# Rows of the split activations at one start modulo 256 bytes, in a hybrid decoder step on one core

## The chip, the cores and the metric

The kernel runs on one core of one Trainium2 chip. The metric is device time in microseconds (us), the median of several runs of one program. Engines are named as in the profile: PE is TensorE (matmuls), PEld its weight loads, DVE VectorE, ACT ScalarE, POOL GpSimd, SP SyncE, which here only issues DMAs.

## What is computed

The reference is one step of a decoder layer for 256 prompt tokens and 8 sample tokens (one new token of each of 8 requests), which share all weights. Everything is float32. Cut to its projections, it is:

```python
proj = rms_norm(x, g_mix) @ w_in                      # 2048 -> 6656: q, k, v, z, xBC, dt
attn = window_attention(q, k, v, sinks)               # window 128, 16 heads of 64, 4 kv heads
ssd  = rms_norm(scan(conv(xBC), dt) * silu(z), norm_g)
x = x + concat([attn, ssd]) @ w_out                   # 3072 -> 2048
x = x + cross_attention(x, memory) @ w_co             # 4 heads of 128 over 256 memory tokens
u = conv3(rms_norm(x, g_ffn) @ w_up)                  # 2048 -> 2 x 5632
x = x + (silu(gate(u)) * value(u)) @ w_down           # 5632 -> 2048
```

It also returns the new states and caches (keys, values, convolution rows, the scan's state).

## The kernel before, in words

**Layout.** Activations are kept transposed: 128 features in the partitions, and the T = 264 tokens (256 prompt, 8 sample) along the row. A block of 128 features is one row of 264 floats, 1,056 bytes. Eight such rows make a tile of 8 x 264 floats, 8,448 bytes, which `T3` allocates.

**Split operands.** A float32 product is computed as three matmuls of the type float32r. Each operand is split in a high half (a copy rounded to that type) and a low half (what is left). For weights this is done in `weights`: SP loads 1,024 columns of raw weights (`wraw`, 512 KB), ACT makes `whi` (L85), DVE makes `wlo` (L86). For activations `split` does it, with ACT and DVE (L93 without a gain, L94 and L95 with one). `mm3` issues the three matmuls: high weights with the high row (L100), high weights with the low row (L101), low weights with the high row (L102). The weights are the stationary operand, 128 columns, and the row of 264 tokens is the moving one.

**The loop.** `proj` takes weights of 8 feature blocks a unit, in two parts. Within a part it goes over the output blocks m (two, in some stages four), and for each over the rows k of the part, three matmuls each. With two output blocks a part has four rows: the order is rows 0 to 3 for m = 0, rows 0 to 3 for m = 1, then rows 4 to 7 for both.

**The stages**, in the order of PE's work: an opening written out by hand (L240), in which PE takes 4 output blocks at once, so that one row is the moving operand of 4 matmuls in a row, or of 8 with its low half; the input projections, with attention and scan between them; the output projection over the attention rows (`AT`) and the scan rows (`Y`); queries, memory keys and memory values; `w_co`; and the feed-forward stage, in which the up-projection (`up`, rows `X2`) runs one group of 8 blocks ahead of the down-projection (`down`, rows `H`). In the opening, rows 0 to 5 of a pass come one by one (four matmuls with the high half, four with the low half, both on high weights, then four with the high half on low weights), and later rows in pairs.

**Where the rows lie.** The split activations live in the pool `apool` under two tags of four buffers each, "A" and "B": xh, xl (input), yh, yl (scan output), ath, atl (attention output), x1h, x1l (for the queries), ohl (cross-attention output, high rows 0 to 3 and low rows 4 to 7 of one tile), x2h, x2l (up-projection), hh, hl (down-projection). In the built program all these buffers start at 192 modulo 256, because a buffer of 8,448 bytes is 33 x 256. A row is 4 x 256 + 32 bytes long, so the row k of a tile starts at 192 + 32k modulo 256. The buffers of `whi` and `wlo` start at 192 modulo 256 too, and a slice of 128 columns is 512 bytes.

The split memory rows (`mh`, `ml`, 256 tokens) are not under these tags: the first eight high rows are a T3 tile that starts at 192, with rows 1,056 bytes apart, and the other eight and all low rows are 1,024 bytes apart and start at 160 modulo 256.

**Software DMAs.** DMAs that POOL issues need a scratch in SBUF; the program reserves 16,384 bytes of each partition for it. POOL issues the loads of the samples' scan states (`h`, L868, three buffers) and of a broadcast (`cb`, L865) between 160 and 390 us, and the stores of new states (`hn`, L1333) in the feed-forward stage. All other DMAs are issued by SP.

**What sets the order.** A tile framework places the instructions on the engines by priorities, and the kernel pins some by `issue_after` and, in the opening, by hand.

Of the kernel before, what the change touches and what calls it, by code (L numbers as in the profile page):

```python
# [7 lines left out]
F32 = mybir.dt.float32  # L8
F32R = mybir.dt.float32r
# [6 lines left out]
KB = D // 128  # L16
TP, TS = 256, 8
T = TP + TS
EPS = 1e-6
DFF = 5632  # L20
FB = DFF // 128
# [26 lines left out]
def hybrid_decoder_step_kernel(ctx: ExitStack, tc: tile.TileContext, I, O):  # L48
    nc = tc.nc
# [4 lines left out]
    apool = ctx.enter_context(tc.tile_pool(name="apool", bufs=1))  # L54
# [7 lines left out]

    def T3(pool, n, dt=F32, tag=None, name=None, bufs=None):
        return pool.tile([128, n, T], dt, tag=tag, name=name or tag, bufs=bufs)


    NPART, WBUFS = 1024, 4
# [22 lines left out]
    def split(hi, lo, x, g=None):  # L90

        if g is None:
            return S.copy(out=hi, in_=x), V.tensor_tensor(out=lo, in0=x, in1=hi.bitcast(F32), op=ALU.subtract)  # L93
        return (S.activation(out=hi, in_=x, func=AF.Copy, scale=g),  # L94
                V.scalar_tensor_tensor(out=lo, in0=x, scalar=g, in1=hi.bitcast(F32), op0=ALU.mult, op1=ALU.subtract))  # L95
# [7 lines left out]

    def proj(units, acts, evac, n=T, nb=2, tag="mm"):

# [25 lines left out]
    par = cpool.tile([128, NPC], F32, name="par")  # L131
    cst = cpool.tile([128, NCST], F32, name="cst")
    hcol = cpool.tile([32, 2], F32, name="hcol")
    wdt = T3(apool, 8, F32, "C", "wdt").rearrange("p a t -> p (a t)")[:, 0:512].rearrange("p (k c) -> p k c", c=32)
    w_in = I["w_in"]
    small = ctx.enter_context(tc.tile_pool(name="small", bufs=2))
    A = []
    for h in range(2):
        A.append((T3(apool, 8, F32R, "A", f"xh{h}", 4), T3(apool, 8, F32R, "A", f"xl{h}", 4)))

# [1 line left out]
    op = oc.enter_context(tc.tile_pool(name="op", bufs=1))  # L144
    BLK = T + 512
    quarter = [op.tile([128, (KB if q == 0 else 0) + 4 * BLK], F32, name=f"open{q}") for q in range(4)]
# [9 lines left out]
    def x_of(k):  # L156
        return blocks[k // 4][:, k % 4, 0:T], gmix[:, k:k + 1]

# [12 lines left out]
    def w_piece(k, n):  # L171
        if k % 2 == 0:
            pre[k // 2] = [wpool.tile([128, NPART], F32R, tag=t, name=t, bufs=WBUFS).rearrange("p (k c) -> p k c", c=512)
                           for t in ("whi", "wlo")]
        return blocks[k // 4][:, k % 4:k % 4 + n, T:], *(w[:, k % 2:k % 2 + n, :] for w in pre[k // 2])

# [9 lines left out]

    acc0 = small.tile([128, T], F32, tag="acc", bufs=1, name="acc0")
    table = small.tile([128, 1], F32, tag="r", bufs=2, name="table")
# [74 lines left out]
    def pc(name, i=0, n=1):  # L263
        o = _PC[name][0]
        return par[:, o + i:o + i + n]
# [7 lines left out]
    eps = cpool.tile([128, 1], F32, name="eps")  # L273
    V.memset(eps, EPS)

# [9 lines left out]
    def sumsq(acc, x, first, w=T, on=P):  # L285
        if first:
            S.activation(out=acc, in_=x, func=AF.Square)
        else:
            sq = small.tile([128, T], F32, tag="sq", name="sq")
            S.activation(out=sq[:, :w], in_=x, func=AF.Square)  # L290
            on.tensor_tensor(out=acc, in0=acc, in1=sq[:, :w], op=ALU.add)
# [587 lines left out]
        V.tensor_tensor(out=x, in0=x, in1=pc("d_skip", 4 * g, 4).unsqueeze(2).broadcast_to([128, 4, 8]), op=ALU.mult)  # L879


    Y = [(T3(apool, 8, F32R, "B", f"yh{h}", 4), T3(apool, 8, F32R, "B", f"yl{h}", 4)) for h in range(2)]
    accy = small.tile([128, T], F32, tag="acc", bufs=1, name="accy")

    def z_pair(i):
# [9 lines left out]
        for m in range(2):  # L895
# [7 lines left out]
            sumsq(accy[:, :TP], y, k == 0, TP, V)  # L903
            split(Y[k // 8][0][:, k % 8, :TP], Y[k // 8][1][:, k % 8, :TP], y, gssd[:, k:k + 1])

    def gate_sample():
# [13 lines left out]
        for h in range(2):  # L920
            split(Y[h][0][:, :, TP:T], Y[h][1][:, :, TP:T], ysam[:, 8 * h:8 * h + 8, :])

# [26 lines left out]


    res_load()
    AT = (T3(apool, 8, F32R, "A", "ath", 4), T3(apool, 8, F32R, "A", "atl", 4))
    with tc.high_priority():
        for j in (0, 4):
            split(AT[0][:, j:j + 4, :], AT[1][:, j:j + 4, :], attn[:, j:j + 4, :])
    w_out = I["w_out"]

    for i in range(8):
        def ev(m, pm, i=i):
            k = 2 * i + m  # L960
            x = res[k // 4][:, k % 4, :]
            V.tensor_tensor(out=x, in0=pm, in1=x, op=ALU.add)
        proj([w_out[i]], [AT], ev, tag="t" if i % 2 else "mm")
        if i == 0:
# [51 lines left out]
    def mem_hl(k):  # L1016
        return mh[k // 8][:, k % 8, :TP], ml[k // 4][:, k % 4, :]

    X1 = [(T3(apool, 8, F32R, "A", f"x1h{h}", 4), T3(apool, 8, F32R, "A", f"x1l{h}", 4)) for h in range(2)]
    accx = small.tile([128, T], F32, tag="acc", bufs=1, name="accx")  # L1020
    for i in range(8):
        def ev(m, pm, i=i):
# [4 lines left out]
            V.tensor_tensor(out=x, in0=t, in1=x, op=ALU.add)  # L1027
            marks["x1"] = split(X1[k // 8][0][:, k % 8, :], X1[k // 8][1][:, k % 8, :], x, pc("g_cross", k))
        proj([w_out[8 + 2 * i], w_out[9 + 2 * i]], Y, ev, tag="t" if i % 2 else "mm")

# [44 lines left out]
    def q_pair(i):  # L1075
# [4 lines left out]

        proj([I["w_cq"][2 * i], I["w_cq"][2 * i + 1]], X1, ev)
        ms = slice(2 * i, 2 * i + 2)
# [162 lines left out]
    for b in range(6):  # L1245
        nc.sync.dma_start(out=va[b // 2][:, b % 2], in_=I["mv"][b])
        vts.append(va[b // 2][:, b % 2])
    OHL = T3(apool, 8, F32R, "A", "ohl", 4)
    OH, OL = OHL[:, 0:4, :], OHL[:, 4:8, :]
    sample_probs()  # L1250
    for b in range(6, 8):
# [13 lines left out]
            heads = out_head(2 * i + m)  # L1265
    nc.sync.dma_start(out=O["mem_v"], in_=vx)

    X2 = [(T3(apool, 8, F32R, "B", f"x2h{h}", 4), T3(apool, 8, F32R, "B", f"x2l{h}", 4)) for h in range(2)]
    accx2 = small.tile([128, T], F32, tag="acc", bufs=1, name="accx2")

    def x2_ev(k, pm):
        x = res[k // 4][:, k % 4, :]
        V.tensor_tensor(out=x, in0=pm, in1=x, op=ALU.add)
        split(X2[k // 8][0][:, k % 8, :], X2[k // 8][1][:, k % 8, :], x, pc("g_ffn", k))


    outs = [psum(t) for t in ("mm", "mm", "t", "t")]
    for pi, (wh, wl) in enumerate(weights(I["w_co"][0])):
        wh, wl = (w.rearrange("p (k c) -> p k c", c=512) for w in (wh, wl))
        for k in range(2):  # L1280
            h = 2 * pi + k
# [7 lines left out]
    for u in range(1, 4):  # L1289
        with tc.issue_after(heads[0].ins), tc.issue_after(heads[1].ins):  # L1290
            proj([I["w_co"][u]], [(OH, OL)], lambda m, pm, u=u: x2_ev(4 * u + m, pm), nb=4,
                 tag=[cyc[(4 * (u - 1) + m) % 5] for m in range(4)])
# [54 lines left out]
    w_up, w_dn = I["w_up"], I["w_dn"]  # L1347

    def up(g):
        H = (T3(apool, 8, F32R, "A", f"hh{g}", 4), T3(apool, 8, F32R, "A", f"hl{g}", 4))  # L1350
        n = len(groups[g])
        for ii, i in enumerate(groups[g]):
            us = []

            def ev(m, pm, i=i):
                bi = i + FB * m
                u = fp.tile([128, 2 + T], F32, tag="u", name="u", bufs=4)
                P.memset(u[:, 0:2], 0.0)
                ffn["ev"] = V.tensor_tensor(out=u[:, 2:], in0=pm, in1=r2, op=ALU.mult)
                us.append(u)  # L1360

            proj([w_up[2 * i], w_up[2 * i + 1]], X2, ev, tag="t" if i % 2 else "mm")
            cs = []
            for m in range(2):
                bi = i + FB * m
                u = us[m]
                ffn["new"] = P.tensor_copy(out=fnew[:, bi, :], in_=u[:, TP:])
                c = fp.tile([128, TP], F32, tag="c", name="c", bufs=4)
                w = [pc("fw", t * 88 + bi) for t in range(3)]
                ffn["c"] = S.activation(out=c, in_=u[:, 0:TP], func=AF.Identity, scale=w[0], bias=pc("fb", bi))  # L1370
                for t in (1, 2):
                    V.scalar_tensor_tensor(out=c, in0=u[:, t:t + TP], scalar=w[t], in1=c, op0=ALU.mult, op1=ALU.add)
                cs.append(c)
            if i < 4:
                past(i)
            if 4 <= i < 36:
                with tc.issue_after(ffn["ev"].ins), tc.issue_after(ffn["c"].ins):
                    new_state(i // 2 - 2, i % 2)
            S.activation(out=cs[0], in_=cs[0], func=AF.Silu)
            V.tensor_tensor(out=cs[1], in0=cs[0], in1=cs[1], op=ALU.mult)  # L1380
            split(H[0][:, ii, :TP], H[1][:, ii, :TP], cs[1])
        b0 = groups[g][0]
        sc = []
        for m in range(2):
            bi = b0 + FB * m
            t = fp.tile([128, 8, 8], F32, tag="sc", name="sc", bufs=4)[:, 0:n, :]
            P.tensor_tensor(out=t, in0=fnew[:, bi:bi + n, 2:10], in1=pc("fw", 2 * 88 + bi, n).unsqueeze(2).broadcast_to([128, n, 8]), op=ALU.mult)
            P.tensor_tensor(out=t, in0=t, in1=fpc[:, bi:bi + n, :], op=ALU.add)
            sc.append(t)
        S.activation(out=sc[0], in_=sc[0], func=AF.Silu)  # L1390
        V.tensor_tensor(out=sc[1], in0=sc[0], in1=sc[1], op=ALU.mult)
        split(H[0][:, 0:n, TP:T], H[1][:, 0:n, TP:T], sc[1])
        return H

    def down(g, H, last):
        if len(groups[g]) == 8:
# [3 lines left out]
        for src, nb, b0 in plan:  # L1400
            def ev(m, pm, b0=b0):
# [3 lines left out]
                if last:  # L1405
                    nc.sync.dma_start(out=O["y"][:, k, :], in_=x)
            proj([src], [H], ev, nb=nb)

# [148 lines left out]
def build(shapes):  # L1557

    import concourse.bacc as bacc

    nc = bacc.Bacc("TRN2", target_bir_lowering=False, num_devices=1)
    ins = {n: nc.dram_tensor(f"in_{n}_dram", s, dt, kind="ExternalInput").ap() for n, (s, dt) in shapes.items()}
    outs = {n: nc.dram_tensor(f"out_{n}_dram", s, F32, kind="ExternalOutput").ap() for n, s in _OUTS}
    with tile.TileContext(nc, schedule_with_timeline_sim=True) as tc:
        hybrid_decoder_step_kernel(tc, ins, outs)
    return nc
# [10 lines left out]
```

## Time and profile before

| | us |
|---|---|
| runs: median of 3 (lowest to highest) | 1399.39 (1399.31 to 1399.88) |
| profiled execution: span from the first to the last instruction | 1397.1 |
| PE busy (matmuls, 11,535) | 1392.5 |
| DVE busy | 1052.1 |
| ACT busy | 769.3 |
| POOL busy | 95.4 |

The profiled execution is an execution of its own; its span leaves out what lies before the first and after the last instruction, and the median of the runs is 2.3 us above it.

How to read the rows: a window's row has its bounds in us, its length, the engine's busy time with the number of instructions, the granted share of PE's clock, the mean busy share of the DMA engines, and GB/s. A row in order of time has the start in us, how long it took, engine, line, operation, output and inputs, the shape, and how many equal instructions it merges. A group's row has busy us and mean ns of one, then the idle time ahead of it and what ended that.

Successive matmuls overlap: one is marked as lasting some 284 ns, but the next starts some 121 ns after it did. What counts for time is the step from start to start, which is time divided by the number of starts.

### The profile page before, as it was taken

Reading aid. Unit: us, or ns where it says so; the run is one execution under the profiler, and the core shown is the slowest. Engines: PE = TensorE matmul, PEld = TensorE weight load, DVE = VectorE, ACT = ScalarE, POOL = GpSimd, SP = SyncE. Lnnn points to the kernel's source line nnn. Section 1 sums busy time; section 2 is a strip of 40 time slices with the busy share of each in tenths; the row PEclk is TensorE's granted clock in tenths of the full one; section 3 lists DMA queues with packets and bytes.
Section 4 is the critical chain, followed back from the end, with each engine's and each line's share of the span. In section 5 each row is a group of like instructions: output and inputs, shape, how many; then the busy total and the mean of one; then the engine's idle time right before and its main releaser. Section 6 shows DMA issues by size and latency. Waiting matters only on the chain.

```text
span 1397.1 us, 29012 instructions
## 1 busy us (share of the span) xinstructions
PE 1392.5 (100%) x11535; PEld 1367.8 (98%) x11535; DVE 1052.1 (75%) x1874; ACT 769.3 (55%) x1255; POOL 95.4 (7%) x286
## 2 busy tenths in 40 slices
PE   9999999999999999999999999999999999999999
PEld 9999999999999999899999999999999999999998
DVE  7879799999987774578777775777577757765654
ACT  7667756556545554566565544554455445543532
POOL 0000011121000000002010000000000000000000
PEclk9999999999999999999999999999999999999999
DMA  7954467777777567565576765676567656655664
GB/s 299 323 162 135 139 217 245 233 239 253 235 221 240 182 237 263 209 251 191 186 255 213 255 208 187 211 254 211 185 211 239 197 184 197 196 180 183 191 185 138
DMA packets 89479, 298.33 MB, mean 214 GB/s; under 512 B 12032, under 2 KB 17152, under 8 KB 88832
## 3 DMA queue, kind: packets, MB, share of 16 engines
q1 hardware_dynamic: 83840, 277.61, 60.5%
q0 software_dynamic: 5504, 18.88, 4.1%
q8 instruction: 90, 1.47, 0.4%
q14 instruction: 45, 0.37, 0.1%
HBM read 280.77 MB, written 16.23 MB: 213 GB/s over the span
## 4 chain that ended last, share of the span: by engine, by line
PE 100%; DVE 0%; issue 0%
PE mm L100 21%; PE mm L101 21%; PE mm L102 21%; PE t L100 10%; PE t L102 10%; PE t L101 10%; PE t L240 1%; PE y L825 1%; PE t L278 1%; PE y L841 0%; PE s L240 0%; PE mm L240 0%; PE x L278 0%; PE t L559 0%; PE x L1137 0%; PE s L1184 0%
## 5 line engine op out<-in xcount | busy, mean ns | idle before, releaser
L85 ACT CAST whi<-wraw 128x1024 fp32r<-128x1024 f32 x440 | 459.9, 1048 | 530.6 <-PE mm L101 278.3
L86 DVE TENSOR_TENSOR wlo<-wraw,whi 128x1024 fp32r<-128x1024 f32 x440 | 541.8, 1233 | 221.1 <-ACT whi L85 217.3
L100 PE MATMUL mm<-x2h,whi 128*128 128x264 f32 x704 | 199.8, 284 | 0.0
L100 PE MATMUL t<-x2h,whi 128*128 128x264 f32 x704 | 199.8, 284 | 0.0
L102 PE MATMUL t<-x2h,wlo 128*128 128x264 f32 x704 | 199.7, 284 | 0.0
L101 PE MATMUL mm<-x2l,whi 128*128 128x264 f32 x704 | 199.6, 284 | 0.0
L101 PE MATMUL t<-x2l,whi 128*128 128x264 f32 x704 | 199.5, 283 | 0.0
L102 PE MATMUL mm<-x2h,wlo 128*128 128x264 f32 x704 | 199.3, 283 | 0.0
L101 PE MATMUL mm<-hl,whi 128*128 128x264 f32 x704 | 198.7, 283 | 0.0
L102 PE MATMUL mm<-hh,wlo 128*128 128x264 f32 x704 | 198.2, 283 | 0.0
L100 PE MATMUL mm<-hh,whi 128*128 128x264 f32 x704 | 197.2, 284 | 0.0
L100 PE MATMUL mm<-xh,whi 128*128 128x264 f32 x576 | 164.7, 287 | 0.0
L101 PE MATMUL mm<-xl,whi 128*128 128x264 f32 x576 | 164.5, 287 | 0.0
L102 PE MATMUL mm<-xh,wlo 128*128 128x264 f32 x576 | 162.8, 287 | 0.0
L101 PEld LDWEIGHTS mm<-x2l,whi 128*128 128x128 f32 x704 | 132.6, 188 | 0.0
L100 PEld LDWEIGHTS t<-x2h,whi 128*128 128x128 f32 x704 | 132.5, 188 | 0.0
L101 PEld LDWEIGHTS t<-x2l,whi 128*128 128x128 f32 x704 | 132.5, 188 | 0.0
L101 PEld LDWEIGHTS mm<-hl,whi 128*128 128x128 f32 x704 | 132.4, 188 | 0.0
L100 PEld LDWEIGHTS mm<-x2h,whi 128*128 128x128 f32 x704 | 132.4, 188 | 0.0
L102 PEld LDWEIGHTS t<-x2h,wlo 128*128 128x128 f32 x704 | 132.2, 188 | 0.0
L102 PEld LDWEIGHTS mm<-x2h,wlo 128*128 128x128 f32 x704 | 132.1, 188 | 0.0
L102 PEld LDWEIGHTS mm<-hh,wlo 128*128 128x128 f32 x704 | 132.0, 188 | 0.0
(506 smaller groups left out, 2950.7 us busy)
## 6 DMA issues: line engine op xcount, KB each, us to landing
wraw<-in_w_up_dram SPq DMA_DIRECT2D x176, 512.0 KB, 4.4
wraw<-in_w_in_dram SPq DMA_DIRECT2D x96, 512.0 KB, 4.7
wraw<-in_w_dn_dram SPq DMA_DIRECT2D x88, 512.0 KB, 4.3
wraw<-in_w_out_dram SPq DMA_DIRECT2D x48, 512.0 KB, 4.4
h<-in_h_dram POOLq DMA_DIRECT2D x32, 256.0 KB, 4.6
hn<-in_h_dram SPq DMA_DIRECT2D x16, 512.0 KB, 4.8
out_state_s_dram<-hn POOLq DMA_DIRECT2D x16, 512.0 KB, 3.5
e<-dram_la SPq DMA_DIRECT2D x16, 256.0 KB, 5.5
```

Source lines behind the costliest of these rows:

```text
L85: S.copy(out=hi, in_=x)
L86: V.tensor_tensor(out=lo, in0=x, in1=hi.bitcast(F32), op=ALU.subtract)
L100: PE.matmul(out, wh, xh, start=start, stop=False)
L101: PE.matmul(out, wh, xl, start=False, stop=False)
L102: return PE.matmul(out, wl, xh, start=False, stop=stop)
L240: PE.matmul(first[c][:, :T], pre[k // 2][i][:, k % 2, c * 128:(c + 1) * 128], A[k // 8][x][:, k % 8, :], start=k + i + x == 0, stop=k == K ...
L278: return PE.transpose(out, in_, cst[0:k, C_ID:C_ID + k])
L825: PE.matmul(y[o:o + 64, (h // 2) * 128:(h // 2) * 128 + 128], xdt[:, h, :], es[h // 4][:, h % 4, :], start=True, stop=True)
```

## The change

Three edits:

- A helper `rows` takes the place of `T3` for all split activations under the tags "A" and "B". It allocates 8 rows of 320 floats, 1,280 bytes or 5 x 256, and hands out the first 264 of each. All rows of a tile now start at the same place modulo 256. A buffer grows from 8,448 to 10,240 bytes, eight buffers by 14,336 together. Other tiles under these tags (caches, flat scratch) keep their size and lie at the front of a buffer.
- An unused tile of 56 floats (224 bytes) is allocated first in `apool`, so that the buffers behind it, tag "C" among them, start at 160 modulo 256 in place of 192.
- The scratch of the software DMAs shrinks from 16,384 to 2,048 bytes a partition: 14,336 bytes, 56 x 256. The weight buffers therefore stay at 192 modulo 256.

In the built program every row of xh, xl, yh, yl, ath, atl, x1h, x1l, ohl, x2h, x2l, hh and hl starts at 160 modulo 256. Tiles that lie behind these buffers move down by 32 modulo 256 (the memory rows from 160 to 128). The instructions of every engine stand in the same order as before. Only four have another shape: the two splits of the attention rows write 4 rows of 264 on ACT and DVE where they wrote one run of 1,056.

```diff
+PITCH = 320
...
+    def rows(tag, name):
+        return apool.tile([128, 8, PITCH], F32R, tag=tag, name=name, bufs=4)[:, :, :T]
...
     hcol = cpool.tile([32, 2], F32, name="hcol")
+    apool.tile([128, 56], F32, tag="gap", name="gap")
     wdt = T3(apool, 8, F32, "C", "wdt").rearrange("p a t -> p (a t)")[:, 0:512].rearrange("p (k c) -> p k c", c=32)
...
-        A.append((T3(apool, 8, F32R, "A", f"xh{h}", 4), T3(apool, 8, F32R, "A", f"xl{h}", 4)))
+        A.append((rows("A", f"xh{h}"), rows("A", f"xl{h}")))
...
-    Y = [(T3(apool, 8, F32R, "B", f"yh{h}", 4), T3(apool, 8, F32R, "B", f"yl{h}", 4)) for h in range(2)]
+    Y = [(rows("B", f"yh{h}"), rows("B", f"yl{h}")) for h in range(2)]
...
-    AT = (T3(apool, 8, F32R, "A", "ath", 4), T3(apool, 8, F32R, "A", "atl", 4))
+    AT = (rows("A", "ath"), rows("A", "atl"))
...
-    nc = bacc.Bacc("TRN2", target_bir_lowering=False, num_devices=1)
+    nc = bacc.Bacc("TRN2", target_bir_lowering=False, num_devices=1, dynamic_dma_scratch_size=2048)
```

The same replacement is made for x1h and x1l, ohl, x2h and x2l, and hh and hl.

More of the change, by code (lines that the diff above doesn't have):

```diff
@@ L1017, in mem_hl @@
         return mh[k // 8][:, k % 8, :TP], ml[k // 4][:, k % 4, :]
-    X1 = [(T3(apool, 8, F32R, "A", f"x1h{h}", 4), T3(apool, 8, F32R, "A", f"x1l{h}", 4)) for h in range(2)]
+    X1 = [(rows("A", f"x1h{h}"), rows("A", f"x1l{h}")) for h in range(2)]
     accx = small.tile([128, T], F32, tag="acc", bufs=1, name="accx")
@@ L1247, in hybrid_decoder_step_kernel @@
         vts.append(va[b // 2][:, b % 2])
-    OHL = T3(apool, 8, F32R, "A", "ohl", 4)
+    OHL = rows("A", "ohl")
     OH, OL = OHL[:, 0:4, :], OHL[:, 4:8, :]
@@ L1266, in hybrid_decoder_step_kernel @@
     nc.sync.dma_start(out=O["mem_v"], in_=vx)
-    X2 = [(T3(apool, 8, F32R, "B", f"x2h{h}", 4), T3(apool, 8, F32R, "B", f"x2l{h}", 4)) for h in range(2)]
+    X2 = [(rows("B", f"x2h{h}"), rows("B", f"x2l{h}")) for h in range(2)]
     accx2 = small.tile([128, T], F32, tag="acc", bufs=1, name="accx2")
@@ L1349, in up @@
     def up(g):
-        H = (T3(apool, 8, F32R, "A", f"hh{g}", 4), T3(apool, 8, F32R, "A", f"hl{g}", 4))
+        H = (rows("A", f"hh{g}"), rows("A", f"hl{g}"))
         n = len(groups[g])
```

## The prediction

> **What bounds the kernel now.** I read the page first, then PE's waits, then the windows of the feed-forward stage, and last the single instructions in order of time.
>
> ```profile
> span 1397.1 us, 29012 instructions
> PE 1392.5 (100%) x11535; PEld 1367.8 (98%) x11535; DVE 1052.1 (75%) x1874; ACT 769.3 (55%) x1255; POOL 95.4 (7%) x286
> PEclk9999999999999999999999999999999999999999
> PE 100%; DVE 0%; issue 0%
> ```
>
> PE is busy for all of the span, the chain that ended last is PE alone, and the granted clock is in its top tenth in every slice. PE's waits are one row:
>
> ```profile
> PE x L201 <- DVE eps L274: 1.2, 1, 1.2
> ```
>
> So no transfer and no other engine holds PE back; only the pace at which matmul follows matmul counts. A row of the page does not give that pace, because matmuls overlap:
>
> ```profile
> L100 PE MATMUL mm<-x2h,whi 128*128 128x264 f32 x704 | 199.8, 284 | 0.0
> ```
>
> One takes 284 ns, but its successor starts long before it ends. The pace is time by count, over a window of the feed-forward stage in which PE runs nothing but matmuls of 264 columns (first row PE, second DVE, third DVE in the input projections):
>
> ```profile
> 650.00:1390.00 740.00, 740.00 (x6113) 1.00 0.63 204
> 650.00:1390.00 740.00, 512.01 (x833) 1.00 0.63 204
> 30.00:360.00 330.00, 300.92 (x638) 1.00 0.66 216
> ```
>
> 740.00 us over 6,111 starts (of the 6,113, two were already running at the window's edge) is 121.1 ns a matmul, at clock 1.00. DVE is busy for 69% of the first window, but for 91% of the second.
>
> **What each part costs.** Before, row k of an activation tile starts at 192 + 32k modulo 256, so rows 0 to 7 start at 192, 224, 0, 32, 64, 96, 128, 160, and every pass over a tile goes through all eight. After, every row starts at 160. The slices of the weights start at 192 modulo 256 in both kernels. The term that decides is therefore the pace of a stream whose rows all start at 160. The trace holds a small piece of it: in the opening (L240) row 7 is the moving operand of eight matmuls in a row, four of xh and four of xl, on four slices of weights. Two such pieces, the two halves of the opening:
>
> ```profile
> 15.41 0.41 PE L240 MATMUL t<-xh,whi 128*128 128x264 f32 x2
> 15.66 0.28 PE L240 MATMUL mm<-xh,whi 128*128 128x264 f32 x1
> 15.78 0.28 PE L240 MATMUL s<-xh,whi 128*128 128x264 f32 x1
> 15.90 0.40 PE L240 MATMUL t<-xl,whi 128*128 128x264 f32 x2
> 16.14 0.28 PE L240 MATMUL mm<-xl,whi 128*128 128x264 f32 x1
> 16.26 0.28 PE L240 MATMUL s<-xl,whi 128*128 128x264 f32 x1
> ...
> 27.08 0.41 PE L240 MATMUL t<-xh,whi 128*128 128x264 f32 x2
> 27.33 0.28 PE L240 MATMUL mm<-xh,whi 128*128 128x264 f32 x1
> 27.45 0.28 PE L240 MATMUL s<-xh,whi 128*128 128x264 f32 x1
> 27.57 0.40 PE L240 MATMUL t<-xl,whi 128*128 128x264 f32 x2
> 27.81 0.28 PE L240 MATMUL mm<-xl,whi 128*128 128x264 f32 x1
> 27.93 0.28 PE L240 MATMUL s<-xl,whi 128*128 128x264 f32 x1
> ```
>
> The first two steps after row 6 take 0.25 us together in both pieces (15.41 to 15.66, 27.08 to 27.33): an entry. The five steps behind it take 0.60 us in both, 120.0 ns each, unbroken by the change from xh to xl in their middle. Another start in the same opening gives another pace; row 4, which starts at 64, has eleven steps from its first to its twelfth matmul:
>
> ```profile
> 11.50 0.42 PE L240 MATMUL t<-xh,whi 128*128 128x264 f32 x2
> ...
> 12.86 0.29 PE L240 MATMUL s<-xh,wlo 128*128 128x264 f32 x1
> ```
>
> 1.36 us over 11 is 123.6 ns. I take it from these rows that the start does matter, that a stream which stays at 160 settles at 120.0 ns, and that the entry is paid only where the start changes. After the change it no longer changes.
>
> **The pace rule of the Trainium skill.** Its page "TensorE: Matmul & The Clock Gate", section "Back-to-back issue gap", puts matmuls in a stream N / 2.4 + 2.5 ns apart when warm, with no term for where a row starts. For 264 columns that is 112.5 ns by estimate; this trace has 121.1, so the measurement decides on the size. By that formula the pace term would be zero.
>
> *The sum.* Matmuls of 264 columns outside the opening: up-projection 88 blocks x 16 rows x 3 = 4,224, down-projection 44 x 16 x 3 = 2,112, input projections 48 x 16 x 3 = 2,304, output projection 16 x 24 x 3 = 1,152, query projection 4 x 16 x 3 = 192, w_co 16 x 4 x 3 = 192: 10,176. Each gains 121.1 - 120.0 = 1.1 ns, in all 11.2 us. The opening's own 192 I leave out; its first matmuls keep the pace of the loads. The sum is made on the profiled execution: 1397.1 - 11.2 = 1385.9 us of span. The median of the runs, 1399.39, lies 2.3 us above that span, and I carry this over: 1388.2 us.
>
> *Its bounds.* A start is printed to 0.01 us, so ten steps in 1.20 us are 118.6 to 121.4 ns, a gain of 25 us at one end and a loss of 3 at the other. I take the middle, because two pieces 12 us apart agree. The 2,304 matmuls of the input projections are the least sure, since DVE is already busy 91% of that stretch: if DVE became late there, their 2.5 us would be lost. In the feed-forward stage DVE's cover is 31% and PE gains 1%, so it stays hidden; DMA is busy for 0.63 there.
>
> *The splits of the attention rows (L955, recorded as L93).* Two ACT and two DVE instructions now write four rows of 264 with gaps, where each wrote 1,056 in one run.
>
> ```profile
> L93 ACT CAST ath<-attn x2: 1072/1072/1072, 358.4 to 359.4; 128x1056 fp32r<-128x1056 f32 x2
> L93 ACT CAST hh<-c 128x256 fp32r<-128x256 f32 x44 | 17.7, 402 | 1.3 <-DVE c L1380 1.3
> ```
>
> As four separate copies of nearly a row they would take 4 x 402 = 1,608 ns, so the break between rows costs from nothing to 0.5 us each, on engines that PE does not wait for. I take nothing, with 2 us if all four were exposed. All other writers already write one row, or the eight sample columns of each.
>
> *The scratch.* It shrinks from 16,384 to 2,048 bytes a partition. The software queue carries what POOL issues and nothing else: 32 loads and 8 of 256 KB and 16 stores of 512 KB make its 18.9 MB.
>
> ```profile
> q0 software_dynamic: 5504, 18.88, 4.1%
> L868 POOL DMA_DIRECT2D h<-in_h_dram x32 | 17.4, 543 | 141.1 <-DVE ych L870 100.6 <-PE mm L102 20.4 <-DVE cnew L741 18.6
> DMA to landing us min/median/max: 3.6/4.6/7.0
> DVE h L869: 0.6, 1
> ```
>
> POOL already stands still for 141.1 us until a tile h is free, and three such tiles exist, so at most three of these loads are open at a time, next to one of cb. If each of the 32 also had to wait for its forerunner to land, that would be 32 x 4.6 = 147 us, nearly all of it inside the 141.1 that POOL waits anyway; up to 6 us could reach DVE, which takes h, with the low halves of the weights queued behind it. DVE waited 0.6 us for h in all. I take nothing and keep 6 us for the range. No gain comes from here.
>
> **The rivals.**
>
> *A, the forecast:* the stream settles at 120.0 ns; 1388.2 us; chance 0.62. By the parts above its own range is 1380 to 1396.
>
> *B, the start is not the cause.* The steps would differ by their order in the pass, and their mean would be kept. The memory-key projection speaks for this. It streams 256 columns; its first 48 matmuls take their high halves from rows at eight different starts, the next 48 have every operand's rows at 160. Its first matmul, the first on the second tile, and the first of the next stage:
>
> ```profile
> 510.01 0.28 PE L100 MATMUL mm<-mh,whi 128*128 128x256 f32 x1
> ...
> 515.69 0.28 PE L100 MATMUL mm<-mh,whi 128*128 128x256 f32 x1
> ...
> 521.37 0.29 PE L100 MATMUL mm<-x1h,whi 128*128 128x264 f32 x1
> ```
>
> 5.68 us over 48 is 118.3 ns, 5.68 over 48 the same. Against it: those rows are shorter and end elsewhere, and a third of the first 48, the low halves, start at 160 too. It gives 1399.4; chance 0.19. The Trainium skill's page "SBUF — State Buffer", section "Specifications (TRN2)", says that memory lines have 16 bytes and that two hits a line keep full bandwidth. By that rule all starts here, multiples of 32 bytes, would be alike, and the time B's; the two paces of the opening, 120.0 and 123.6, do not fit it.
>
> *C, 160 is a bad start inside a projection.* In the feed-forward stage row 7's three matmuls are high, low, high, on changing weights, and one visit is slow:
>
> ```profile
> 705.81 0.29 PE L100 MATMUL mm<-x2h,whi 128*128 128x264 f32 x1
> 705.94 0.28 PE L101 MATMUL mm<-x2l,whi 128*128 128x264 f32 x1
> 706.06 0.28 PE L102 MATMUL mm<-x2h,wlo 128*128 128x264 f32 x1
> 706.18 0.28 PE L100 MATMUL mm<-x2h,whi 128*128 128x264 f32 x1
> ```
>
> 0.37 us over three is 123.3 ns. If that were the pace of every row, not the price of coming from row 6, the loss would be 2.2 x 10,176 = 22 us, 1421.8. With half of the visits at the mean it is 11 us, 1410.6, which I give for C. It decides where the settled pace at 160 lies above 121.1. Against it stand the five even steps of 120.0; chance 0.19. A scratch that makes POOL late would add its 6 us here.
>
> **How the numbers follow.** The likeliest case gives 1388.2. The range takes A from 1380 (a pace of 119.2) and B whole, and reaches 1406, the near part of C; most of C and a tail of A are left out, near 2 in 10. A measurement of this kernel can tell about 0.2%, 2.8 us, from no change: A is faster, B the same, C slower, which gives 0.62, 0.19 and 0.19.
>
> **What would show it.** Right: the window 650 to 1390 counts about 6,167 matmuls (740 / 0.120), all steps alike in runs, and the gain grows evenly along PE's stream, 7 us of it in the feed-forward stage. B: still 6,113. C: fewer, about 6,060. DVE waiting for h, or PE waiting for low halves of weights between 160 and 400 us, would show the scratch. It is wrong if the pace moves in the up-projection alone, since all stages share the starts.

## The result, and the profile after

| | before | after |
|---|---|---|
| runs, median of 5, us (lowest to highest) | 1399.48 (1399.31 to 1399.88) | 1388.36 (1387.37 to 1388.79) |
| profiled execution, span, us | 1397.1 | 1386.1 |

The ratio is 0.992, 95% interval 0.9908 to 0.9932: 11.1 us less, where 11.2 were forecast. The page of the changed kernel:

```profile
span 1386.1 us, 29012 instructions
PE 1381.1 (100%) x11535; PEld 1355.9 (98%) x11535; DVE 1050.2 (76%) x1874; ACT 768.4 (55%) x1255; POOL 96.7 (7%) x286
PEclk9999999999999999999999999999999999999999
PE 97%; DVE 1%; DMA 1%; ACT 1%; issue 0%; SPq 0%; ACTq 0%; DVEq 0%
```

The same instructions ran at the same clock, and the other engines were busy as long as before, to within 2 us; PE's busy time fell by 11.4 us. The chain that ended last is no longer PE alone: 3% of it now goes over DVE, DMA and ACT.

The windows, PE first and DVE second, of the feed-forward stage and of the stretch with the input projections (the feed-forward window ends at 1380, since this kernel's last matmul starts at 1382.45):

```profile
650.00:1380.00 730.00, 730.00 (x6086) 1.00 0.63 206
650.00:1380.00 730.00, 508.16 (x827) 1.00 0.63 206
30.00:360.00 330.00, 301.24 (x640) 1.00 0.67 218
```

730 us over 6,084 starts (two were already running at the edge) is 119.99 ns a step; the kernel before has 6,031 in the same window, 121.1 ns:

```profile
650.00:1380.00 730.00, 730.00 (x6031) 1.00 0.64 205
```
The steps themselves, in order of time in the up-projection:

```profile
700.02 0.28 PE L104 MATMUL mm<-x2h,whi 128*128 128x264 f32 x1
700.13 0.28 PE L105 MATMUL mm<-x2l,whi 128*128 128x264 f32 x1
700.25 0.28 PE L106 MATMUL mm<-x2h,wlo 128*128 128x264 f32 x1
700.38 0.28 PE L104 MATMUL mm<-x2h,whi 128*128 128x264 f32 x1
...
701.10 0.28 PE L104 MATMUL mm<-x2h,whi 128*128 128x264 f32 x1
```

They repeat every three matmuls, 0.36 us, whichever row, weights or output block it is: nine steps in 1.08 us. Before, the step depended on the place in the pass, as in the 0.37 us that the prediction shows for row 7's three.

Where the gain lies is read from the same landmark in both traces. The rows are the chain's first group behind the opening, the first matmul of the output projection, the first of the feed-forward stage, and the last matmul. Of the kernel before:

```profile
29.19 1.93 PE x L247 x32
362.95 0.41 PE L100 MATMUL mm<-ath,whi 128*128 128x264 f32 x2
625.82 0.29 PE L100 MATMUL mm<-x2h,whi 128*128 128x264 f32 x1
1393.43 0.28 PE L102 MATMUL mm<-hh,wlo 128*128 128x264 f32 x1
```

and of the changed one:

```profile
28.91 1.92 PE x L252 x32
360.72 0.40 PE L104 MATMUL mm<-ath,whi 128*128 128x264 f32 x2
621.71 0.36 PE L104 MATMUL mm<-x2h,whi 128*128 128x264 f32 x1
1382.45 0.28 PE L106 MATMUL mm<-hh,wlo 128*128 128x264 f32 x1
```

0.3 us were gained in the opening, 3.8 from there to the feed-forward stage (2.0 of them in the input projections), and 6.9 in it. The 0.3 in the opening are not shown to be the rows' doing, since run 1 below, whose rows lie as before, has them too:

```profile
28.91 1.93 PE x L247 x32
```

### The profile page after: what moved, and what is told of

Read it like the earlier page. It is cut to its first block, busy times and chain, and to the rows that moved or that the text cites. A ratio compares the mean times of both kernels' runs of the same rounds, so it can differ in the third digit from the quotient of the medians.

```text
span 1386.1 us, 29012 instructions
## 1 busy us (share of the span) xinstructions
PE 1381.1 (100%) x11535; PEld 1355.9 (98%) x11535; DVE 1050.2 (76%) x1874; ACT 768.4 (55%) x1255; POOL 96.7 (7%) x286
## 4 chain that ended last, share of the span: by engine, by line
PE 97%; DVE 1%; DMA 1%; ACT 1%; issue 0%; SPq 0%; ACTq 0%; DVEq 0%
PE mm L105 21%; PE mm L106 21%; PE mm L104 21%; PE t L105 10%; PE t L106 9%; PE t L104 9%; PE t L245 1%; PE t L283 1%; PE y L830 1%; PE y L846 0%; DMA e<-dram_la 0%; DMA open<-in_open_dram 0%; PE mm L245 0%; PE s L245 0%; PE t L564 0%; PE x L1142 0%
## 5 line engine op out<-in xcount | busy, mean ns | idle before, releaser
L104 PE MATMUL mm<-x2h,whi 128*128 128x264 f32 x704 | 196.5, 279 | 0.0
L104 PE MATMUL t<-x2h,whi 128*128 128x264 f32 x704 | 196.4, 279 | 0.0
L104 PE MATMUL mm<-hh,whi 128*128 128x264 f32 x704 | 194.1, 280 | 0.0
```

Of the source, the lines that this page charges most:

```text
L104: PE.matmul(out, wh, xh, start=start, stop=False)
```

## The experiments

The prediction left open what in the starts matters. The theories tested:

- **S**: each start has a settled pace of its own, which can be read from a few matmuls in the opening. This is the step on which the forecast rests.
- **O**: one start for all rows is what counts, whichever it is.
- **R** against **A2**: what counts is the row's start relative to that of the weights, or the row's own.
- **L**, formed after the first four runs: a stream with one start locks into a repeating cycle of steps; several cycles exist, 120.0 ns is the fastest, and a slower one can hold until PE pauses.

All paces below are from the window 650 to 1380 (two instructions less than its count), where PE runs nothing but matmuls of 264 columns.

**1. The scratch alone.**

```diff
-    nc = bacc.Bacc("TRN2", target_bir_lowering=False, num_devices=1)
+    nc = bacc.Bacc("TRN2", target_bir_lowering=False, num_devices=1, dynamic_dma_scratch_size=2048)
```

> The kernel before, with the smaller scratch alone; every row starts where it did modulo 256. If the gain is the pace of the matmuls, nothing moves: 1399.5 us, 121.1 ns a step in the feed-forward stage. If the scratch has any part in the time, by POOL's loads or by where tiles lie in memory, the time leaves 1399.5 by more than 1 us; the full gain would be 1388.4.

```profile
650.00:1380.00 730.00, 730.00 (x6030) 1.00 0.64 205
```

1399.34 us, ratio 1.0 (0.9991 to 1.0009), 121.1 ns. The scratch has no part in the time that shows, to 0.1%.

**2. The gap alone.** The scratch is small (run 1's edit), the gap is there, rows stay 1,056 bytes apart.

```diff
+    apool.tile([128, 56], F32, tag="gap", name="gap")
```

> The kernel before with the gap and the smaller scratch, rows still 1,056 bytes apart: a tile goes through the same eight starts, rotated by one (160, 192, 224, 0 and then 32 to 128). Both theories of the pace (each start has its own; or only the change from start to start costs) expect the mean over all eight to stay: 121.1 ns, 1399.5 us, at most 3 us from it, since the rows that follow each other at the ends of a part are others. If the gap as such is the gain, 1388.

```profile
650.00:1380.00 730.00, 730.00 (x6040) 1.00 0.64 206
```

1397.8 us, ratio 0.999 (0.9981 to 1.0), 120.9 ns. Rotating the eight starts moves the mean by 0.2 ns. The gap alone is not the gain.

**3. Rows at 192: the change without its gap.**

```diff
-    apool.tile([128, 56], F32, tag="gap", name="gap")
```

> The change without its gap: rows 1,280 bytes apart, all at 192 modulo 256. Theory S (each start has a settled pace of its own): in the opening of the kernel before, row 0 of the second half took 0.60 us over the five steps from 17.61 to 18.21, 120.0 ns, so 1388, within 6 us for the rounding of the rows. Theory O (one start for all is what counts, whichever): 1388.4, the time of the changed kernel. This run alone does not part them; it tells whether 160 is needed.

The ten executions fall into two groups: five from 1389.96 to 1391.16 and five from 1398.63 to 1400.05 (the profiled one, at 1400.05). Median 1394.9, ratio 0.9965 (0.9944 to 0.9985), which describes neither group.

```profile
650.00:1380.00 730.00, 730.00 (x6019) 1.00 0.64 205
```

In the profiled execution, of the slower group, the pace is 121.3 ns. No trace of the other group was kept; that its pace is lower is read from its time alone. One program then has two paces, so one start does not have one settled pace: S and O both miss. The gap is needed if every execution is to have the gain. L was formed on this and the next run.

**4. Rows at 64.**

```diff
-    apool.tile([128, 56], F32, tag="gap", name="gap")
+    apool.tile([128, 32], F32, tag="gap", name="gap")
```

> The changed kernel with a gap of 128 bytes in place of 224: all rows at 64 modulo 256. Theory S: row 4 in the opening of the kernel before, which starts there, had 123.6 ns a step over eleven steps, so 2.5 ns over the mean of 121.1, times 10,176 is 25 us more than before: 1425 us, slower than before. Theory O: 1388.4, like 160. Theory B of the prediction (starts do not matter) has fallen with the result, unless it was the distance and not the start.

1393.16 us, ratio 0.9957 (0.9942 to 0.9972): 32 us less than S had forecast, 5 more than O. The stage changes its pace within itself. It begins at 73 starts in 9 us, 123.3 ns, close to the 123.6 of row 4 in the opening. At 641.40 two matmuls with other operands (L300, a sum for the norm) stand in the stream; the next two rows begin 0.25 and 0.56 us behind that, and a few matmuls later the stream runs at 120.0:

```profile
630.00:639.00 9.00, 9.00 (x75) 1.00 0.70 226
650.00:1380.00 730.00, 730.00 (x6086) 1.00 0.64 206
```

The timeline at the change of pace, in which the second row is the break:

```profile
641.27 0.29 PE L105 MATMUL t<-x2l,whi 128*128 128x264 f32 x1
641.40 0.61 PE L300 MATMUL y<-accx,cst 128*128 128x264 f32 x2
641.65 0.48 PE L106 MATMUL t<-x2h,wlo 128*128 128x264 f32 x1
641.96 0.28 PE L104 MATMUL t<-x2h,whi 128*128 128x264 f32 x1
```

**5. Rows at 192 and weights at 224.** A tile of 32 bytes ahead of the weights moves them by 32; the gap of 224 behind them brings the rows back to 192.

```diff
+    cpool.tile([128, 8], F32, name="wgap")
     apool.tile([128, 56], F32, tag="gap", name="gap")
```

> Rows at 192 as in the run without the gap (which fell into two groups, five executions near 1390 and five near 1399), but the weights moved from 192 to 224 modulo 256, so that rows and weights stand to each other as in the changed kernel (rows 32 bytes behind). Theory R (what counts is the start of the moving row relative to the weights that load beside it): the changed kernel's time in every execution, 1388.4, 120.0 ns a step. Theory A2 (what counts is the row's own start): again two groups, 1390 and 1399.

```profile
650.00:1380.00 730.00, 730.00 (x6086) 1.00 0.64 206
```

1387.18 us in the median of executions from 1386.92 to 1388.29, ratio 0.9914 (0.9899 to 0.9929), 120.0 ns. The rows start where run 3 had them; of the operands of the projections, only the weights moved, by 32 bytes. Four executions could miss a slower group (1 chance in 16 at run 3's shares), but all four also lie below run 3's faster group, which begins at 1389.96. R fits this, A2 does not. It is the only place where one relative start was tried at two absolute ones.

**6. Two starts in turn: rows 1,152 bytes apart, at 160 and 32.**

```diff
-PITCH = 320
+PITCH = 288
```

> Rows 1,152 bytes apart (4.5 x 256), so that they start at 160 and at 32 in turn. If a change of start costs an entry at each row (the prediction's reading): at least the mean of the kernel before, 121.1 ns and 1399.5 us, since the start changes as often as there and 12.5 ns of entry over six steps would make it 122. If any short repeating pattern of starts locks into a cycle at the floor of 120.0: 1388.4.

```profile
650.00:1380.00 730.00, 730.00 (x6028) 1.00 0.64 205
```

1399.85 us, ratio 1.0005 (0.9995 to 1.0014), 121.1 ns, the time of the kernel before. Half of the rows at 160 bring nothing, with the other half at the start that run 12 shows to be the slowest. With run 12 (all rows at 32, 126.7 ns), the mean of the two single paces would be 123.3; the pair takes 121.1, so paces of starts do not add up.

**7. Rows at 128.** The gap has 48 floats.

> Gap of 192 bytes, all rows at 128. Theory S (settled pace read in the opening of the kernel before, here 14.69 to 15.29, 0.60 us over five steps): 120.0 ns, 1388. Theory L (one start for all locks the stream into some cycle; 120.0 is the fastest, slower ones exist and hold until PE pauses): 1388 to 1393, by stage 120.0 or a steady slower value such as the 121.3 and 123.3 that rows at 192 and 64 showed; never a changing mean like 121.1 of eight starts.

```profile
650.00:1380.00 730.00, 730.00 (x6085) 1.00 0.64 206
```

1390.65 us, ratio 0.9938 (0.9923 to 0.9952), 120.0 ns here. The 2.3 us over the changed kernel lie ahead of this window: the profiled execution begins its feed-forward stage at 624.79, the changed kernel's at 621.71. L's range holds it, S's point lies 2.7 us below.

**8. Rows at 96.** The gap has 40 floats.

> Gap of 160 bytes, all rows at 96. The opening of the kernel before had 122.7 ns a step there (12.98 to 14.33, eleven steps). Theory S: 1.6 ns x 10,176 = 16 us over before, 1416. Theory L: stages at 120.0 and stages at a steady slower value near 122, so between 1388 and 1409; in the feed-forward stage 120.0 once PE has paused.

```profile
650.00:1380.00 730.00, 730.00 (x6002) 1.00 0.64 205
```

1404.97 us, ratio 1.0039 (1.0024 to 1.0054): one start for all rows, and slower than eight. The pace is 121.7 ns; the same two matmuls of L300 stand in this stream (at 643.07) and did nothing to it: 74 starts in the 9 us from 630 are 121.6 ns. That goes against L's guess of 120.0 behind them.

**9. Rows at 224.** The gap has 8 floats.

> Gap of 32 bytes, all rows at 224, 32 bytes ahead of the weights modulo 256. Theory S: in the opening of the kernel before row 1, which starts there, took 1.10 us over the nine steps from 7.24 to 8.34, 122.2 ns: 1.1 x 10,176 = 11 us over before, 1411. Theory L (a cycle is steady, which one depends on start and on how the stream began): each stage at 120.0 or at one steady slower value, so 1388 to 1411, and the feed-forward stage at one value from its first pause on.

```profile
650.00:1380.00 730.00, 730.00 (x5975) 1.00 0.63 204
```

1409.51 us, ratio 1.0071 (1.0058 to 1.0085), 122.2 ns, as S read it in the opening.

**10. Rows at 0.** The gap has 16 floats.

> Gap of 64 bytes, all rows at 0, 64 bytes ahead of the weights. Theory S: row 2 in the opening of the kernel before, 8.84 to 9.92, 1.08 us over nine steps, 120.0 ns with an error of 1 ns: 1388, within 11. Theory L: each stage at 120.0 or at one steady slower value; 1388 to 1400.

```profile
650.00:1380.00 730.00, 730.00 (x6037) 1.00 0.64 206
```

Two groups again, four executions from 1390.17 to 1391.16 and six from 1395.71 to 1397.79; median 1396.01, ratio 0.9963 (0.9949 to 0.9976). The profiled one, of the second group, has 121.0 ns.

**11. The memory rows at one start.** In the changed kernel, with the first eight high rows of the memory 1,024 bytes apart and at 128, like its other memory rows.

```diff
-    mh = [T3(apool, 8, F32R, "C", "mh0"), xp.tile([128, 8, TP], F32R, name="mh1")]
+    mh = [T3(apool, 8, F32R, "C", "mh0").rearrange("p a t -> p (a t)")[:, 56:2104].rearrange("p (k t) -> p k t", t=TP), xp.tile([128, 8, TP], F32R, name="mh1")]
```

> The changed kernel with the first eight high rows of the memory 1,024 bytes apart and at 128, like the other memory rows there (64 bytes behind the weights). In the changed kernel the second 48 matmuls of the memory keys, whose rows all start at 128, step at 113 to 114 ns, the first 48, whose high rows go through eight starts, at 118. If one start for all is what counts there too, the first half of the keys and values, 192 matmuls, gains 4 to 5 ns each: 0.8 to 1.0 us, 1387.5, which may not come clear of the noise; the windows of the memory stage then show 113.3 ns throughout.

1388.11 us (1387.86 to 1388.61), ratio 0.9918 (0.9904 to 0.9931): no gain that can be told from the changed kernel's 1388.36. The keys, from their first matmul to the first of the next stage, in this run and then in the changed kernel:

```profile
506.55 0.28 PE L104 MATMUL mm<-mh,whi 128*128 128x256 f32 x1
...
512.20 0.28 PE L104 MATMUL mm<-mh,whi 128*128 128x256 f32 x1
...
517.86 0.29 PE L104 MATMUL mm<-x1h,whi 128*128 128x264 f32 x1
```

```profile
506.48 0.28 PE L104 MATMUL mm<-mh,whi 128*128 128x256 f32 x1
...
512.15 0.28 PE L104 MATMUL mm<-mh,whi 128*128 128x256 f32 x1
...
517.59 0.28 PE L104 MATMUL mm<-x1h,whi 128*128 128x264 f32 x1
```

In the changed kernel the first 48 take 5.67 us, 118.1 ns, and the second, at one start, 5.44, 113.3. With one start throughout, all 96 take 11.31 us, 117.8 ns. The second 48 start at the same places in both programs and take 5.44 and 5.66 us, some 4.5 ns a step apart, so what ran ahead of them decides their pace. This fits L: the stream locked into a slower cycle at its beginning and stayed in it, while the changed kernel came into the fast one by way of the mixed rows.

**12. Rows at 32.** The gap has 24 floats.

> Gap of 96 bytes, all rows at 32, 96 bytes ahead of the weights. Theory S: row 3 in the opening of the kernel before, 10.28 to 11.38, 1.10 us over nine steps, 122.2 ns: 1411. Theory L: each stage at 120.0 or at one steady slower value; 1388 to 1411. There the steps were uneven, so that this is the start where I least know which cycle holds.

```profile
650.00:1380.00 730.00, 730.00 (x5764) 1.00 0.61 198
```

1450.3 us, ratio 1.0363 (1.0349 to 1.0377): 51 us slower than before. The pace is 126.7 ns, where S had read 122.2 in the opening, and it holds through the stage. The time lies far above the range that I had given for L.

The map, with the row's start relative to the weights' (modulo 256):

| row relative to weights | rows / weights at | ns a step, feed-forward | us |
|---|---|---|---|
| -32 | 160 / 192 | 120.0 | 1388.4 |
| -32 | 192 / 224 | 120.0 | 1387.2 |
| -64 | 128 / 192 | 120.0 | 1390.7 |
| -128 | 64 / 192 | 123.3, then 120.0 | 1393.2 |
| 0 | 192 / 192 | 121.3 in the profiled one | 1390 or 1400 |
| 64 | 0 / 192 | 121.0 in the profiled one | 1391 or 1397 |
| -96 | 96 / 192 | 121.7 | 1405.0 |
| 32 | 224 / 192 | 122.2 | 1409.5 |
| 96 | 32 / 192 | 126.7 | 1450.3 |
| all eight in turn | before | 121.1 | 1399.5 |

That the first column is what counts rests on the first two rows alone; all others left the weights at 192. The period of 256 fits the runs: neighbouring rows of the changed kernel, 1,280 bytes apart, alternate modulo 512 and step alike, while starts 128 apart, 160 and 32, differ by 6.7 ns. All these rows are equally long, so no run here tells a row's start from its end.

## Why the prediction was right, point by point

- **PE's pace bounds the kernel.** Right. Everything that moved the pace moved the time with it, in both directions.
- **121.1 to 120.0 ns on 10,176 matmuls, 11.2 us.** Right: 119.99 measured, 11.0 us between the spans. By stage: 6.9 us in the feed-forward stage against 6,336 x 1.1 = 7.0, and 2.0 in the input projections against 2.5. The opening's 0.3, which I had left out, hides part of that shortfall. The bounds of the reading were drawn too narrow: two pieces of 0.60 us whose starts are all rounded to 0.01 us allow 118.0 to 122.0 ns, not 118.6 to 121.4.
- **"A stream which stays at 160 settles at 120.0 ns."** Right for 160, and the cycle of three that the opening's trace has there, 121, 122 and 117 ns, is the one that now runs. But the way to it, S, is not a method: read from the same opening, 64 should have been 123.6 and ended at 120.0, and 32 should have been 122.2 and was 126.7. A few steps show one cycle out of several, after one way of entering it. Read in the same way, to 0.01 us, the opening gave 120.0 for the starts 192, 0 and 128 too, and the first two of these turned out to have two groups. That 160 holds the fast cycle in every execution seen was therefore not to be read from two pieces: that part of the forecast was luck.
- **"The entry is paid only where the start changes."** The runs leave this open: two starts in turn take 121.1, more than 160 alone and less than the mean of the two, 123.3. It does not follow that no change is fast; at 96, 224 and 32 a single start is slower than the eight in turn.
- **"The start does matter", and the weights are at 192 in both.** I gave the weights a sentence and no part. Run 5 shows that they have one: with the rows at 192, moving the weights by 32 bytes brought the changed kernel's time. That the two reads disturb each other in memory fits this, but no run here shows the mechanism. The Trainium skill's page "TensorE: Matmul & The Clock Gate", section "Step-by-step: what each phase is for", says that matmul rows and weight loads have ports of their own and that loading the next weights takes no read bandwidth from the running matmul. With nothing shared the weights' start should not matter, yet moving it alone took the time from 1390 or 1400 us to 1387.2; whether read bandwidth is what they share, no run here shows.
- **The pace rule of the Trainium skill.** At clock 1.00 the streams took 120.0 to 126.7 ns, against the estimate of 112.5, so the formula has neither the size nor the spread. The prediction also read more into it than the section that it names says: "Back-to-back issue gap" in the Trainium skill's page "TensorE: Matmul & The Clock Gate" calls this formula the gap of an isolated matmul; that warm back-to-back matmuls keep it stands elsewhere on that page.
- **Rival B** (the start is not the cause) fell. Its evidence was a coincidence: the memory rows at 160 had happened to take 118.3, the mean of the mixed rows; at 128, in the changed kernel, they run at 113.3. What the prediction drew from the 16-byte lines in the Trainium skill's page "SBUF — State Buffer", section "Specifications (TRN2)", that all starts here would be alike, falls with it: 120.0 to 126.7 ns.
- **Rival C** did not happen at 160; the 123.3 ns of row 7 in the kernel before belonged to the mixed stream, and which neighbour causes it no run shows. That one start for all can be a bad one is real: at 32 it costs 51 us.
- **The scratch.** Costed at nothing, rightly: run 1 has a ratio of 1.0.
- **The splits of the attention rows.** Costed at nothing, rightly, out of 0 to 0.5 us a break. ACT's two still take 1,072 ns, and DVE's two take 1,248, 4 more than before (first row before, second after):

```profile
L93 DVE TENSOR_TENSOR atl<-attn,ath x2: 1243/1244/1244, 362.8 to 365.1; 128x1056 fp32r<-128x1056 f32 x2
L97 DVE TENSOR_TENSOR atl<-attn,ath x2: 1247/1248/1248, 361.0 to 363.2; 128x1056 fp32r<-128x1056 f32 x2
```

- **DVE's cover in the input projections.** It held but for 0.3 us, and is nearly used up. DVE is busy for 301.24 of 330 us there. Apart from its beginning and the last result, the changed kernel's chain leaves PE just there, and PE has a wait that it did not have before (last row):

```profile
203.14 1.28 DVE h L874 x2
204.43 1.14 DVE wlo L90
...
216.03 5.83 DMA e<-dram_la
221.94 1.36 ACT e L814 x5
...
PE y L830 <- ACT hp L848: 0.3, 1, 0.3
```

A further gain of PE's pace would probably be lost first between 200 and 230 us; no run tests that, and run 5's profile, at the same pace, has no such wait.

## What to carry to other kernels

Where PE is back to back, its pace is a term of its own: count starts in a window, and compare the steps at different places of the pass. If they differ and repeat, try the starts of the moving rows against those of the weights, all of them, since one start for all can be the best or by far the worst, and take one whose executions all agree. A few steps elsewhere in the trace are a hint at such a pace, not its value: a stream can hold several cycles.

## What the runs showed of the hardware that was not expected

- Matmuls of one shape, without any wait, step at 120.0 to 126.7 ns, depending on where the moving row starts modulo 256 bytes while the weights stay at 192. The one relative start that was tried at two places, 32 bytes behind the weights, had 120.0 at both.
- Several such cycles are stable for one program. Behind an interruption by two other matmuls one stream went from 123.3 to 120.0 ns, another kept its 121.7, and at starts 0 and 64 relative to the weights, executions of one program differ by 6 to 9 us in two groups.
- The fastest steady pace seen is 120.0 ns for 264 columns and 113.3 for 256: 6.7 ns for 8 columns, where 264 columns at 120.0 have 0.45 ns each on average.
